# LoRA router, softmax(x @ W): x loaded as float32 by SyncE's queue and converted by ScalarE, weights in few pieces, eight blocks through TensorE at the end

## The chip, the cores and the metric

The kernel runs on one core of a Trainium2 chip. The metric is device time in microseconds (us), the median of several runs. Engines are named as in the profile: PE is TensorE's matmul, PEld its load of the stationary operand, DVE is VectorE, ACT is ScalarE, POOL is GpSimd, SP is SyncE. SPq, ACTq and POOLq are the parts of these engines that issue DMAs. TensorE's granted clock has two levels, 1.2 GHz (0.5 in the profile) and 2.4 GHz (1.0).

## The reference

```python
batch, seq, dim, num_loras = 16, 512, 1024, 8      # x: 33.55 MB of float32
logits = np.matmul(x, router_weights)              # (8192 x 1024) @ (1024 x 8)
exp_logits = np.exp(logits - np.max(logits, axis=-1, keepdims=True))
return exp_logits / np.sum(exp_logits, axis=-1, keepdims=True)
```

## The kernel before

The 8192 rows are split as row = (t, p, g): t is one of T = 4 quarters, p one of 128 partitions, g one of G = 16. A load takes four values of g for one t: 128 partitions x 4 rows x 1024, 2.1 MB of float32 in memory. Four loads (t = 0 to 3) make a group `nb`, and there are NB = 4 groups, so 16 loads in all. The last load (group 3, t = 3) is cut in three (`xl`, two blocks, one, one); a block is one g of one t, 128 rows of x.

x is loaded by POOL's queue, whose DMA converts float32 to bf16 on the way, into nine buffers `xb` (lines 70 to 88); the tenth load waits until a buffer has been read. The weights are loaded by SP's queue (lines 91 to 98): `w_blk` four times, once for each quarter of the partitions, and `w_nat` once. `w_blk` takes word pairs (b, i): partition i holds rows 2 x (32 b + i) and the next, so that each of its 16 pieces is 64 bytes; `w_nat` has eight pieces of 32 bytes on each partition.

DVE then works in the order in which its instructions are written (`tc.manual_schedule`): `wd` is cleared and filled from `w_blk`, `w_bf` from `w_nat`, the identity is copied, `fold` is summed, and after that come the steps for x:

- `turn(nb, t)`: one DVE transpose of 32 x 32 blocks over the whole load, in which a pair of bf16 counts as one float32 word: `xb` to `xt`.
- `logits(nb, nt)`: 32 matmuls with `wd`, in four column strips of TensorE, into `lt`; needs all of the group's transposes.
- `back(nb - 1)`: ACT copies `lt` to `lts`, PE adds the four strips (`po`), and the softmax follows: `mx`, `ex` on DVE, `ev` (Exp) on ACT, `ssum`, `inv`, `outv` on DVE. It is written behind the second transpose of the next group.

The last four blocks go another way: PE transposes each of them in eight steps (`pt`, line 218), DVE copies the result out of PSUM (`xT`, line 220), and `project` multiplies it by `w_bf` in eight steps (line 209) into `lg`. A last softmax and a store by ACT's queue end the kernel.

Of the kernel before, what the change touches and what calls it, by code (L numbers as in the profile page):

```python
# [10 lines left out]
def kernel(  # L11
# [6 lines left out]
    nc = tc.nc  # L18
    P = 128
    B, S, D = x.shape  # L20
    D2, N = router_weights.shape
# [14 lines left out]
    GB = 4  # L36
# [11 lines left out]
    out_tail = out.rearrange("b s n -> (b s) n").rearrange("(t p g) n -> t p g n", t=T, p=P)  # L48
# [5 lines left out]
    xtp = ctx.enter_context(tc.tile_pool(name="xT", bufs=2))  # L54
    sm = ctx.enter_context(tc.tile_pool(name="sm", bufs=2))
    ps_lt = ctx.enter_context(tc.tile_pool(name="ps_lt", bufs=2, space=bass.MemoryType.PSUM))
    ps_out = ctx.enter_context(tc.tile_pool(name="ps_out", bufs=2, space=bass.MemoryType.PSUM))
    ps_t = ctx.enter_context(tc.tile_pool(name="ps_t", bufs=2, space=bass.MemoryType.PSUM))
    ps_lg = ctx.enter_context(tc.tile_pool(name="ps_lg", bufs=1, space=bass.MemoryType.PSUM))

    LAST = NB - 1
    TAIL_LOADS = [2, 1, 1]

    with tc.manual_schedule():

        xs = {}
        tail = []
        ident_bf = const.tile([P, P], bf16)
        ident = const.tile([P, P], fp32)
        for nb in range(NB):  # L70
            for t in range(T):
                if nb == LAST and t == TAIL_T:
                    g = nb * GB
                    for i, r in enumerate(TAIL_LOADS):
                        xb = xtail.tile([P, r, D], bf16, name=f"xl{i}", tag=f"xl{i}")
                        nc.gpsimd.dma_start(out=xb[:], in_=x_v[t, :, g:g + r, :])  # L76
                        tail += [(xb, k) for k in range(r)]
                        g += r
                    continue
                xb = xpool.tile([P, GB, D], bf16, name="xb")  # L80
                if nb == 0 and t == 0:
                    for k in range(GB):
                        nc.gpsimd.dma_start(out=xb[:, k, :], in_=x_v[t, :, k, :])  # L83
                else:
                    nc.gpsimd.dma_start(out=xb[:], in_=x_v[t, :, nb * GB:(nb + 1) * GB, :])  # L85
                xs[nb, t] = xb
                if nb == 0 and t == 0:
                    make_identity(nc, ident)
# [25 lines left out]
        )  # L114

        outv = const.tile([P, Q, G, N], fp32)
        out_t = const.tile([P, GB, N], fp32)

        def softmax(lg, rows, dst, np_):

            shape = [np_] + rows
            ax = X
            mx = sm.tile([P] + rows + [1], fp32, name="mx")
            nc.vector.reduce_max(mx[:np_, ..., 0], lg, axis=ax)  # L124
            ex = sm.tile([P] + rows + [N], fp32, name="ex")
            nc.vector.tensor_tensor(  # L126
                out=ex[:np_], in0=lg, in1=mx[:np_].broadcast_to(shape + [N]), op=ALU.subtract
            )
            ev = sm.tile([P] + rows + [N], fp32, name="ev")
            nc.scalar.activation(ev[:np_], ex[:np_], func=Exp)  # L130
            ssum = sm.tile([P] + rows + [1], fp32, name="ssum")
            nc.vector.reduce_sum(ssum[:np_, ..., 0], ev[:np_], axis=ax)  # L132
            inv = sm.tile([P] + rows + [1], fp32, name="inv")
            nc.vector.reciprocal(inv[:np_], ssum[:np_])  # L134
            nc.vector.tensor_tensor(  # L135
                out=dst, in0=ev[:np_], in1=inv[:np_].broadcast_to(shape + [N]), op=ALU.mult
            )

        xts = {}

        def turn(nb, t):

            if t == 0:
                xts[nb] = tpool.tile([P, T, GB, W], fp32, name="xt")
            nc.vector.transpose(  # L145
                out=xts[nb][:, t].rearrange("p g w -> p (g w)"),
                in_=xs[nb, t][:].rearrange("p g d -> p (g d)").bitcast(fp32),
            )

        def logits(nb, nt):  # L150

            lt = ps_lt.tile([P, T, GB, L], fp32, name="lt")
            xv = xts[nb][:].rearrange("p t g w -> p (t g w)").bitcast(bf16).rearrange(
                "p (t g b l two) -> p t g b l two", t=T, g=GB, b=WB, two=2
            )
# [12 lines left out]

        def back(nb, nt, lt):
            lts = sm.tile([P, GB, T, L], fp32, name="lts")  # L170
            nc.scalar.copy(lts[:, :, 0:nt, :].rearrange("p g t l -> p t g l"), lt[:, 0:nt])  # L171
            po = ps_out.tile([P, GB, Q, N], fp32, name="po")
# [8 lines left out]
            softmax(  # L181
                po[0:nt * L],
                [GB, Q],
                outv[0:nt * L, :, nb * GB:(nb + 1) * GB, :].rearrange("p q g n -> p g q n"),
                nt * L,
            )

        def store(g0, g1, t, eng):
            eng.dma_start(
                out=out_v[t, :, :, g0:g1, :], in_=outv[t * L:(t + 1) * L, :, g0:g1, :]  # L190
            )

        lt = {}
        for nb in range(NB):
            nt = T if nb < LAST else TAIL_T
            for t in range(nt):
                turn(nb, t)
                if t == 1 and nb > 0:
                    back(nb - 1, T, lt.pop(nb - 1))
            lt[nb] = logits(nb, nt)  # L200
        for t in range(T):
            store(0, LAST * GB, t, nc.sync)


        lg = ps_lg.tile([P, GB, N], fp32, name="lg")

        def project(j, xT):
            for ko in range(KO):
                nc.tensor.matmul(  # L209
                    lg[:, j, :], lhsT=xT[:, ko, :], rhs=w_bf[:, ko, :],  # L210
                    start=(ko == 0), stop=(ko == KO - 1),
                )

        pend = None
        for j, (xb, k) in enumerate(tail):
            pt = ps_t.tile([P, KO, P], bf16, name="pt")
            for ko in range(KO):
                nc.tensor.transpose(pt[:, ko, :], xb[:, k, ko * P:(ko + 1) * P], ident_bf[:])  # L218
            xT = xtp.tile([P, KO, P], bf16, name="xT")
            nc.vector.tensor_copy(out=xT[:], in_=pt[:])  # L220
            if pend is not None:
                project(*pend)
            if j == 0:
                back(LAST, TAIL_T, lt.pop(LAST))
                for t in range(TAIL_T):
                    store(LAST * GB, G, t, nc.sync)
            pend = (j, xT)
        project(*pend)
        softmax(lg[:], [GB], out_t[:], P)
        nc.scalar.dma_start(out=out_tail[TAIL_T, :, LAST * GB:G, :], in_=out_t[:])  # L230


# [28 lines left out]
```

## Time and profile before

| | |
|---|---|
| median of 3 runs | 108.58 us (107.95 to 110.44) |
| the profiled execution's own time | 107.87 us |
| its span, first to last instruction | 106.0 us |
| PE, DVE, ACT, POOL busy | 21.7, 44.6, 5.0, 11.9 us |
| memory read, written | 33.72 MB, 0.26 MB |

The profile is of one execution. Its own time is 1.87 us longer than its span, which is what lies ahead of the first and behind the last instruction. Busy time counts compute instructions alone; a DMA's bytes are counted as it writes them, so the loads of x appear there with 16.78 MB (bf16) and in the memory's own row with 33.5 MB (float32).

### The profile page before, as it was taken

The page shows a single profiled execution, that of the slowest core. Times are in us where ns is not written, and L with a number is a line of the kernel's source. Part 1 is how long each engine was busy: PE and PEld are TensorE (multiplying, and loading weights), DVE is VectorE, ACT ScalarE, POOL GpSimd, SP SyncE. Part 2 cuts the span into 40 slices and gives each one's busy share as a digit, 9 for nine tenths or more (in the row PEclk, how much of TensorE's full clock was granted, in tenths as well). Part 3 has the DMA queues.
Part 4 walks back from the last instruction along what each step waited for, and adds up shares of the span by engine and source line. Part 5 has one row for each costly group of instructions (what it writes and reads, how often), then busy time and mean ns, then how long its engine had stood idle before and what let it go on. Part 6 is the DMA issues. An engine that isn't in the chain of part 4 may idle for free.

```text
span 106.0 us, 617 instructions
## 1 busy us (share of the span) xinstructions
PE 21.7 (21%) x224; PEld 12.7 (12%) x224; DVE 44.6 (42%) x52; ACT 5.0 (5%) x10; POOL 11.9 (11%) x27
## 2 busy tenths in 40 slices
PE   0000000000000000000000772039700673099420
PEld 0000000000000000000000332012600222049410
DVE  1210001000000000003999985999289994904750
ACT  4000000000000000000000021000210021002000
POOL 6963100000000000000121127000000000000000
PEclk9999999999999999999999998555555578558855
DMA  2899999999999999992079999999999995300000
GB/s 22 109 194 231 215 215 217 214 214 217 214 214 217 217 211 217 214 214 54 0 102 219 222 201 222 219 207 219 219 207 232 192 207 105 68 7 0 12 6 6
DMA packets 7329, 17.22 MB, mean 162 GB/s; under 512 B 4640, under 2 KB 4640, under 8 KB 5536
## 3 DMA queue, kind: packets, MB, share of 16 engines
q0 software_dynamic: 3024, 16.78, 78.1%
q1 hardware_dynamic: 4160, 0.41, 4.1%
q10 hardware_dynamic: 144, 0.02, 0.1%
q8 instruction: 1, 0.02, 0.1%
HBM read 33.72 MB, written 0.26 MB: 320 GB/s over the span
## 4 chain that ended last, share of the span: by engine, by line
DMA 44%; DVE 28%; PE 19%; ACT 3%; SPq 2%; issue 2%; ACTq 0%; DVEq 0%
DMA w_nat<-in_router_weights_dram 44%; DVE xt L145 19%; PE lt L160 12%; PE po L174 4%; DVE xT L220 2%; PE pt L218 2%; SPq L95 2%; ACT lts L171 2%; ACT ev L130 1%; DVE mx L124 1%; DVE ex L126 1%; DVE ssum L132 1%; DVE inv L134 1%; DVE outv L135 1%; PE lg L209 1%
## 5 line engine op out<-in xcount | busy, mean ns | idle before, releaser
L145 DVE STREAM_TRANSPOSE xt<-xb 128x2048 f32<-128x2048 f32 x15 | 33.3, 2279 | 0.0
L160 PE MATMUL lt<-xt,wd 128*32 128x512 bf16 (+1 forms) x128 | 13.1, 584 | 76.0 <-DVE xt L145 76.0
L160 PEld LDWEIGHTS <-wd 128*32 128x32 bf16 x128 | 4.7, 135 | 81.8 <-issue 52.9
L108 DVE CAST w_bf<-w_nat 128x64 bf16<-128x64 f32 x1 | 0.2, 197 | 31.6 <-DMA w_nat<-in_router_weights_dram 31.6
L85 POOL DMA_DIRECT2D xb<-in_x_dram x14 | 7.4, 534 | 52.7 <-DVE xt L145 50.0
L103 DVE CAST wd<-w_blk 32x256 bf16<-32x256 f32 x4 | 1.3, 324 | 15.2 <-DMA w_blk<-in_router_weights_dram 15.2
L171 ACT COPY lts<-lt 128x512 f32<-128x512 f32 (+1 forms) x4 | 2.2, 558 | 84.4 <-PE lt L160 84.4
L174 PE MATMUL po<-fold,lts 128*128 128x32 f32 (+1 forms) x32 | 5.0, 305 | 2.1 <-ACT lts L171 2.1
L174 PEld LDWEIGHTS po<-fold,lts 128*128 128x128 f32 (+1 forms) x32 | 4.6, 224 | 4.4 <-ACT lts L171 4.4
L220 DVE COPY xT<-pt 128x1024 bf16<-128x1024 bf16 x4 | 2.7, 685 | 4.5 <-PE pt L218 4.5
L218 PE MATMUL pt<-ident_bf,xl 128*128 128x128 bf16 x32 | 3.3, 264 | 0.0
L124 DVE TENSOR_REDUCE mx<-po 128x16 f32<-128x128 f32 (+1 forms) x4 | 1.2, 291 | 3.7 <-PE po L174 3.7
L218 PEld LDWEIGHTS <-xl 128*128 128x128 bf16 x32 | 2.5, 120 | 0.6 <-issue 0.6
L83 POOL DMA_DIRECT2D xb<-in_x_dram x4 | 2.3, 585 | 0.8 <-POOLq L245 0.8
L132 DVE TENSOR_REDUCE ssum<-ev 128x16 f32<-128x128 f32 (+2 forms) x5 | 1.3, 265 | 2.0 <-ACT ev L130 2.0
L130 ACT ACTIVATE ev<-ex 128x128 f32<-128x128 f32 (+2 forms) x5 | 1.5, 293 | 12.7 <-DVE ex L126 12.7
L209 PE MATMUL lg<-w_bf,xT 128*128 128x8 bf16 x32 | 1.5, 170 | 2.1 <-DVE xT L220 2.1
L76 POOL DMA_DIRECT2D xl<-in_x_dram x3 | 1.6, 547 | 0.0
L209 PEld LDWEIGHTS <-xT 128*128 128x128 bf16 x32 | 1.3, 105 | 2.4 <-DVE xT L220 2.4
L171 ACT ACT_TABLE_LOAD x1 | 1.3, 1283 | 0.7 <-PEq L245 0.7
L134 DVE RECIPROCAL inv<-ssum 128x16 f32<-128x16 f32 (+2 forms) x5 | 1.2, 237 | 0.2
L135 DVE TENSOR_TENSOR outv<-ev,inv 128x128 f32<-128x128 f32 (+1 forms) x4 | 1.2, 291 | 0.1
(13 smaller groups left out, 3.8 us busy)
## 6 DMA issues: line engine op xcount, KB each, us to landing
xb<-in_x_dram POOLq DMA_DIRECT2D x14, 1024.0 KB, 18.9
xb<-in_x_dram POOLq DMA_DIRECT2D x4, 256.0 KB, 5.9
xl<-in_x_dram POOLq DMA_DIRECT2D x1, 512.0 KB, 22.7
xl<-in_x_dram POOLq DMA_DIRECT2D x2, 256.0 KB, 24.9
out_dram<-outv SPq DMA_DIRECT2D x4, 48.0 KB, 1.7
w_blk<-in_router_weights_dram SPq DMA_DIRECT2D x4, 32.0 KB, 3.6
out_dram<-outv SPq DMA_DIRECT2D x3, 16.0 KB, 1.5
w_nat<-in_router_weights_dram SPq DMA_DIRECT2D x1, 32.0 KB, 46.7
```

Of the source, the lines that this page charges most:

```text
L83: nc.gpsimd.dma_start(out=xb[:, k, :], in_=x_v[t, :, k, :])
L85: nc.gpsimd.dma_start(out=xb[:], in_=x_v[t, :, nb * GB:(nb + 1) * GB, :])
L124: nc.vector.reduce_max(mx[:np_, ..., 0], lg, axis=ax)
L130: nc.scalar.activation(ev[:np_], ex[:np_], func=Exp)
L132: nc.vector.reduce_sum(ssum[:np_, ..., 0], ev[:np_], axis=ax)
L145: nc.vector.transpose(out=xts[nb][:, t].rearrange("p g w -> p (g w)"), in_=xs[nb, t][:].rearrange("p g d -> p (g d)").bitcast(fp32),)
L160: nc.tensor.matmul(lt[c * L:(c + 1) * L, 0:nt], lhsT=wd[:, b, two, :], rhs=xv[:, 0:nt, :, b, :, two], start=(s < Q), stop=(s >= steps - Q),)
L171: nc.scalar.copy(lts[:, :, 0:nt, :].rearrange("p g t l -> p t g l"), lt[:, 0:nt])
L174: nc.tensor.matmul(po[0:nt * L, g].rearrange("p q n -> p (q n)"), lhsT=lts[:, g, 0:nt, :], rhs=fold[:], start=True, stop=True,)
L209: nc.tensor.matmul(lg[:, j, :], lhsT=xT[:, ko, :], rhs=w_bf[:, ko, :], start=(ko == 0), stop=(ko == KO - 1),)
L218: nc.tensor.transpose(pt[:, ko, :], xb[:, k, ko * P:(ko + 1) * P], ident_bf[:])
L220: nc.vector.tensor_copy(out=xT[:], in_=pt[:])
```

## The change

x is loaded by SP's queue as float32, without conversion, into five buffers `xf` of 2.1 MB. ACT converts each load to bf16 (`cast`, into one of three buffers `xb`) and DVE transposes that. The weights go to ACT's queue, and the words of x are put in another order: pair number (i, b) instead of (b, i), so that `w_blk` has one piece of 1 KB on each partition, and `w_nat` (ki, ko) one of 256 bytes. To match it, the transpose reads words that lie 64 bytes apart, and PE's transposes take columns that lie 16 bytes apart. `TAIL_T` goes from 3 to 2: the last eight blocks (t = 2 and 3 of the last group) go through PE's transposes, ACT converting each block. POOL clears `wd`. `fill` adds matmuls whose result (`spare`) nobody reads: ten ahead of the last group's logits and two behind each of the first five of the eight blocks. The softmax is cut into `peak` (DVE), `power` (ACT) and `share` (DVE), which are written between other steps. All stores are on SP's queue.

```diff
-    TAIL_T = T - 1
+    LAST = NB - 1
+    TAIL_T = 2
...
-    xpool = ctx.enter_context(tc.tile_pool(name="x", bufs=9))
-    xtail = ctx.enter_context(tc.tile_pool(name="xtail", bufs=1))
+    fpool = ctx.enter_context(tc.tile_pool(name="xf", bufs=5))
+    bpool = ctx.enter_context(tc.tile_pool(name="xb", bufs=3))
...
-        wv = router_weights.rearrange("(b i two) n -> i b (two n)", i=L, two=2)
+        wv = router_weights.rearrange("(i b two) n -> i b (two n)", b=WB, two=2)
         for q in range(Q):
-            nc.sync.dma_start(out=w_blk[q * L:(q + 1) * L], in_=wv)
-        nc.sync.dma_start(
-            out=w_nat[:], in_=router_weights.rearrange("(ko ki) n -> ki ko n", ki=P)
+            nc.scalar.dma_start(out=w_blk[q * L:(q + 1) * L], in_=wv)
+        nc.scalar.dma_start(
+            out=w_nat[:], in_=router_weights.rearrange("(ki ko) n -> ki ko n", ko=KO)
         )
...
+        for nb, t, k0, r in loads:
+            xb = fpool.tile([P, GB, D], fp32, name="xf")
+            g = nb * GB + k0
+            nc.sync.dma_start(out=xb[:, 0:r, :], in_=x_v[t, :, g:g + r, :])
...
-        nc.vector.memset(wd[:], 0.0)
+        nc.gpsimd.memset(wd[:], 0.0)
...
+        def cast(nb, t, r=GB):
+            xb = bpool.tile([P, GB, D], bf16, name="xb")
+            for k in range(0, GB, r):
+                src, j = xf[nb, t, k]
+                nc.scalar.copy(xb[:, k:k + r, :], src[:, j:j + r, :])
...
-            nc.vector.transpose(
-                out=xts[nb][:, t].rearrange("p g w -> p (g w)"),
-                in_=xs[nb, t][:].rearrange("p g d -> p (g d)").bitcast(fp32),
-            )
+            for k in range(0, GB, r):
+                nc.vector.transpose(
+                    out=xts[nb][:, t, k:k + r].rearrange("p g b l -> p (g b) l"),
+                    in_=xbs[nb, t][:, k:k + r, :].rearrange("p g d -> p (g d)").bitcast(fp32)
+                    .rearrange("p (g i b) -> p g b i", g=r, i=L),
+                )
...
+            if nb == LAST:
+                fill(10, moving(nb)[:, 0, 0, :, :, 0])
...
-        for j, (xb, k) in enumerate(tail):
+        for j, (t, k) in enumerate(tail):
...
+            nc.scalar.copy(xb[:, k, :], src[:, s, :])
+            xc = xb[:, k, :].rearrange("p (ki ko) -> p ko ki", ko=KO)
...
-                nc.tensor.transpose(pt[:, ko, :], xb[:, k, ko * P:(ko + 1) * P], ident_bf[:])
+                nc.tensor.transpose(pt[:, ko, :], xc[:, ko, :], ident_bf[:])
...
+            if j < len(tail) - 3:
+                fill(2, moving(LAST)[:, 0, 0, :, :, 0])
             if j == 0:
-                back(LAST, TAIL_T, lt.pop(LAST))
+                lts = copy_out(LAST, TAIL_T, lt)
+            if j == 1:
+                sft = back(LAST, TAIL_T, lts)
+            if j == 2:
+                sft.peak()
+            if j == 3:
+                sft.power()
+            if j == 4:
+                sft.share()
```

ACT's program before, its last rows; it has no work on x itself:

```order
L171 COPY lts<-lt 128x4x4x32
L130 ACTIVATE ev<-ex 128x128
L171 COPY lts<-lt 128x3x4x32
L130 ACTIVATE ev<-ex 96x128
L130 ACTIVATE ev<-ex 128x32
L230 DMA out_dram<-out_t 128x32
```

Ahead of these rows stand only the table load and the same pair of copy and Exp, twice.

ACT's program now, its first eight rows (lines 73 and 74 are the weights, line 150 is `cast`, line 196 is the copy of `lt`, line 129 is Exp):

```order
L73 DMA w_blk<-in_router_weights_dram 32x256 x4
L74 DMA w_nat<-in_router_weights_dram 128x64
L150 ACT_TABLE_LOAD
L150 CAST xb<-xf 128x4096 x5
L196 COPY lts<-lt 128x4x4x32
L150 CAST xb<-xf 128x4096
L129 ACTIVATE ev<-ex 128x128
L150 CAST xb<-xf 128x4096 x3
```

The copy of a group's `lt` stands behind the first cast of the next group, and the Exp behind the second; casts that follow wait for both.

ACT's program now, its last rows, from the last group on (line 262 is the cast of one of the last eight blocks):

```order
L150 CAST xb<-xf 128x2048 x2
L196 COPY lts<-lt 128x4x4x32
L150 CAST xb<-xf 128x2048 x2
L129 ACTIVATE ev<-ex 128x128
L262 CAST xb<-xf 128x1024
L196 COPY lts<-lt 128x2x4x32
L262 CAST xb<-xf 128x1024 x3
L129 ACTIVATE ev<-ex 64x128
L262 CAST xb<-xf 128x1024 x4
L129 ACTIVATE ev<-ex 128x64
```

The copy of the last `lt` stands between the first and the second of the eight casts, and the Exp of that group behind the fourth.

DVE's program before, from its last transpose on:

```order
L145 STREAM_TRANSPOSE xt<-xb 128x2048
L220 COPY xT<-pt 128x1024
L124 TENSOR_REDUCE mx<-po 96x16
L126 TENSOR_TENSOR ex<-po,mx 96x128
L132 TENSOR_REDUCE ssum<-ev 96x16
```

The softmax of the last group stands whole behind the first copy out of PSUM.

DVE's program now, from the last two loads that it transposes in halves (line 158 is the transpose, line 268 the copy out of PSUM, lines 120 to 137 the softmax):

```order
L158 STREAM_TRANSPOSE xt<-xb 128x1024 x2
L134 TENSOR_REDUCE ssum<-ev 128x16
L136 RECIPROCAL inv<-ssum 128x16
L137 TENSOR_TENSOR outv<-ev,inv 128x4x4x8
L268 COPY xT<-pt 128x1024 x3
L120 TENSOR_REDUCE mx<-po 64x16
L122 TENSOR_TENSOR ex<-po,mx 64x128
L268 COPY xT<-pt 128x1024 x2
L134 TENSOR_REDUCE ssum<-ev 64x16
```

`mx` and `ex` of the last group, for which ACT's Exp waits, stand behind the third copy out of PSUM.

## Rows read from the trace of the kernel before

**Rows 1.** The page: 40 slices of 2.65 us, DMA's busy tenths and GB/s written.

```profile
DMA  2899999999999999992079999999999995300000
GB/s 22 109 194 231 215 215 217 214 214 217 214 214 217 217 211 217 214 214 54 0 102 219 222 201 222 219 207 219 219 207 232 192 207 105 68 7 0 12 6 6
```

**Rows 2.** The chain that ended last, in order of time: start us, us, what.

```profile
2.75 46.74 DMA w_nat<-in_router_weights_dram
...
50.12 8.81 DVE xt L145 x4
58.97 3.50 PE lt L160 x32
```

**Rows 3.** The waits of all engines: who for whom, us in total, times, longest.

```profile
POOL xb L85 <- DVE xt L145: 50.0, 6, 41.6
```

**Rows 4.** Stretches: length, busy us of each engine, granted clock, DMA share, GB/s written.

```profile
12.00:46.00 34.00, 0.00 (x0) 0.10 (x1) 0.29 (x1) 0.00 (x0) 0.00 (x0) 1.00 1.06 215
...
49.60:53.50 3.90, 0.00 (x0) 0.00 (x0) 3.90 (x5) 0.00 (x0) 0.53 (x1) 1.00 0.00 0
...
56.00:82.00 26.00, 10.07 (x80) 5.23 (x79) 22.19 (x20) 1.79 (x4) 3.69 (x7) 0.68 1.02 214
```

**Rows 5.** The DMA queues: packets, MB written, share of 16 engines' span.

```profile
q0 software_dynamic: 3024, 16.78, 78.1%
```

**Rows 6.** The start in order of time: start us, us, engine, instruction.

```profile
0.74 1.96 SPq L95 DMA_DIRECT2D w_blk<-in_router_weights_dram  x4
1.23 2.27 POOL L83 DMA_DIRECT2D xb<-in_x_dram  x4 [0.78 <-POOLq L245]
2.63 0.44 DVE L103 CAST wd<-w_blk 32x256 bf16<-32x256 f32 x1 [1.23 <-DMA w_blk<-in_router_weights_dram]
3.44 0.26 POOL masks.py:197 MEMSET ident<- 128x128 f32 x1
```

**Rows 7.** Groups by line and shape: busy us, mean ns of one, idle before.

```profile
L130 ACT ACTIVATE ev<-ex 128x128 f32<-128x128 f32 x3 | 0.9, 309 | 6.4 <-DVE ex L126 6.4
L130 ACT ACTIVATE ev<-ex 128x32 f32<-128x32 f32 x1 | 0.2, 229 | 4.5 <-DVE ex L126 4.5
L171 ACT COPY lts<-lt 128x512 f32<-128x512 f32 x3 | 1.8, 585 | 78.3 <-PE lt L160 78.3
L145 DVE STREAM_TRANSPOSE xt<-xb 128x2048 f32<-128x2048 f32 x15 | 33.3, 2279 | 0.0
L112 DVE TENSOR_REDUCE fold<-ident 128x32 f32<-128x128 f32 x1 | 0.4, 364 | 0.0
L132 DVE TENSOR_REDUCE ssum<-ev 128x16 f32<-128x128 f32 x3 | 0.9, 286 | 1.2 <-ACT ev L130 1.2
L218 PEld LDWEIGHTS <-xl 128*128 128x128 bf16 x32 | 2.5, 120 | 0.6 <-issue 0.6
L174 PEld LDWEIGHTS po<-fold,lts 128*128 128x128 f32 x24 | 3.7, 237 | 4.4 <-ACT lts L171 4.4
```

**Rows 8.** The end in order of time: start us, us, engine, instruction.

```profile
92.60 2.75 PE L160 MATMUL lt<-xt,wd 128*32 128x384 bf16 x32 [4.27 <-DVE xt L145]
95.28 1.03 PE L218 MATMUL pt<-ident_bf,xl 128*128 128x128 bf16 x8
...
96.11 0.90 PE L174 MATMUL po<-fold,lts 128*96 128x32 f32 x8
96.35 0.69 DVE L220 COPY xT<-pt 128x1024 bf16<-128x1024 bf16 x1 [3.81 <-PE pt L218]
...
97.50 0.61 PE L218 MATMUL pt<-ident_bf,xl 128*128 128x128 bf16 x8
...
101.67 0.38 PE L209 MATMUL lg<-w_bf,xT 128*128 128x8 bf16 x8 [0.59 <-DVE xT L220]
102.08 0.19 DVE L124 TENSOR_REDUCE mx<-lg 128x4 f32<-128x32 f32 x1 [0.47 <-PE lg L209]
...
103.28 0.19 DVE L135 TENSOR_TENSOR out_t<-ev,inv 128x32 f32<-128x32 f32 x1
```

More of the change, by code (lines that the diff above doesn't have):

```diff
@@ L47 @@
     )
-    out_tail = out.rearrange("b s n -> (b s) n").rearrange("(t p g) n -> t p g n", t=T, p=P)
+    out_tail = out.rearrange("b s n -> (b s) n").rearrange("(t p g) n -> p t g n", t=T, p=P)
     const = ctx.enter_context(tc.tile_pool(name="const", bufs=1))
-    xpool = ctx.enter_context(tc.tile_pool(name="x", bufs=9))
-    xtail = ctx.enter_context(tc.tile_pool(name="xtail", bufs=1))
+    fpool = ctx.enter_context(tc.tile_pool(name="xf", bufs=5))
+    bpool = ctx.enter_context(tc.tile_pool(name="xb", bufs=3))
@@ L59 @@
+    ps_out = ctx.enter_context(tc.tile_pool(name="ps_out", bufs=1, space=bass.MemoryType.PSUM))
+    ps_t = ctx.enter_context(tc.tile_pool(name="ps_t", bufs=4, space=bass.MemoryType.PSUM))
     ps_lg = ctx.enter_context(tc.tile_pool(name="ps_lg", bufs=1, space=bass.MemoryType.PSUM))
-    LAST = NB - 1
-    TAIL_LOADS = [2, 1, 1]
+    ps_f = ctx.enter_context(tc.tile_pool(name="ps_f", bufs=1, space=bass.MemoryType.PSUM))
+    loads = [(nb, t, 0, GB) for nb in range(NB) for t in range(T)]
+    loads[-1:] = [(LAST, T - 1, 0, 2), (LAST, T - 1, 2, 1), (LAST, T - 1, 3, 1)]
@@ L64 @@
     with tc.manual_schedule():
[L66 to L88, printed above, removed]
@@ new lines @@
+        nc.scalar.dma_start(
+            out=w_nat[:], in_=router_weights.rearrange("(ki ko) n -> ki ko n", ko=KO)
+        )
+        xf = {}
+        for nb, t, k0, r in loads:
+            xb = fpool.tile([P, GB, D], fp32, name="xf")
+            g = nb * GB + k0
+            nc.sync.dma_start(out=xb[:, 0:r, :], in_=x_v[t, :, g:g + r, :])
+            for k in range(r):
+                xf[nb, t, k0 + k] = (xb, k)
+        ident = const.tile([P, P], fp32)
+        make_identity(nc, ident)
+        ident_bf = const.tile([P, P], bf16)
@@ L116 @@
         outv = const.tile([P, Q, G, N], fp32)
[L117 to L127, printed above, removed]
-            )
[L129 to L137, printed above, removed]
@@ L139, with __init__, peak, power @@
-        xts = {}
-        def turn(nb, t):
-            if t == 0:
-                xts[nb] = tpool.tile([P, T, GB, W], fp32, name="xt")
-            nc.vector.transpose(
-                out=xts[nb][:, t].rearrange("p g w -> p (g w)"),
-                in_=xs[nb, t][:].rearrange("p g d -> p (g d)").bitcast(fp32),
-            )
+        out_t = const.tile([P, T - TAIL_T, GB, N], fp32)
+        spare = ps_f.tile([P, 512], fp32)
+        class Softmax:
+            def __init__(self, lg, rows, dst, np_):
+                self.lg, self.rows, self.dst, self.np_ = lg, rows, dst, np_
+            def peak(self):
+                n, rows = self.np_, self.rows
+                mx = sm.tile([P] + rows + [1], fp32, name="mx")
+                nc.vector.reduce_max(mx[:n, ..., 0], self.lg, axis=X)
+                self.ex = sm.tile([P] + rows + [N], fp32, name="ex")
+                nc.vector.tensor_tensor(
+                    out=self.ex[:n], in0=self.lg, in1=mx[:n].broadcast_to([n] + rows + [N]),
+                    op=ALU.subtract,
+                )
+            def power(self):
+                self.ev = sm.tile([P] + self.rows + [N], fp32, name="ev")
+                nc.scalar.activation(self.ev[:self.np_], self.ex[:self.np_], func=Exp)
+            def share(self):
+                n, rows = self.np_, self.rows
+                ssum = sm.tile([P] + rows + [1], fp32, name="ssum")
+                nc.vector.reduce_sum(ssum[:n, ..., 0], self.ev[:n], axis=X)
+                inv = sm.tile([P] + rows + [1], fp32, name="inv")
+                nc.vector.reciprocal(inv[:n], ssum[:n])
+                nc.vector.tensor_tensor(
+                    out=self.dst, in0=self.ev[:n], in1=inv[:n].broadcast_to([n] + rows + [N]),
+                    op=ALU.mult,
+                )
@@ L150, in logits @@
         def logits(nb, nt):
             lt = ps_lt.tile([P, T, GB, L], fp32, name="lt")
-            xv = xts[nb][:].rearrange("p t g w -> p (t g w)").bitcast(bf16).rearrange(
-                "p (t g b l two) -> p t g b l two", t=T, g=GB, b=WB, two=2
-            )
+            xv = moving(nb)
             steps = 2 * WB
@@ L167, in logits, with moving, fill, copy_out @@
             return lt
-        def back(nb, nt, lt):
+        def moving(nb):
+            return xts[nb][:].rearrange("p t g b l -> p (t g b l)").bitcast(bf16).rearrange(
+                "p (t g b l two) -> p t g b l two", t=T, g=GB, b=WB, two=2
+            )
+        def fill(n, rhs, k=None):
+            for _ in range(n):
+                nc.tensor.matmul(
+                    spare[:], lhsT=w_fill, rhs=rhs, start=True, stop=True
+                )
+        w_fill = wd[:, 0:2].rearrange("p b two n -> p (b two n)")
+        def copy_out(nb, nt, lt):
             lts = sm.tile([P, GB, T, L], fp32, name="lts")
             nc.scalar.copy(lts[:, :, 0:nt, :].rearrange("p g t l -> p t g l"), lt[:, 0:nt])
+            return lts
+        def back(nb, nt, lts):
             po = ps_out.tile([P, GB, Q, N], fp32, name="po")
@@ L180, in back @@
                 )
-            softmax(
+            return Softmax(
                 po[0:nt * L],
@@ L196 @@
             for t in range(nt):
[L197 to L200, printed above, removed]
+                r = 2 if nb == LAST else GB
+                cast(nb, t, r)
+                if lt is not None:
+                    if t == 0:
+                        sft = back(nb - 1, T, copy_out(nb - 1, T, lt))
+                    if t == 1:
+                        sft.power()
+                turn(nb, t, r)
@@ L201 @@
+                if lt is not None:
+                    if t == 0:
+                        sft.peak()
+                    if t == 1:
+                        sft.share()
+                        lt = None
+            if nb == LAST:
+                fill(10, moving(nb)[:, 0, 0, :, :, 0])
+            lt = logits(nb, nt)
         for t in range(T):
-            store(0, LAST * GB, t, nc.sync)
-        lg = ps_lg.tile([P, GB, N], fp32, name="lg")
-        def project(j, xT):
+            store(t, 0, LAST * GB)
@@ L208, in project @@
+        tail = [(t, k) for t in range(TAIL_T, T) for k in range(GB)]
+        lg = ps_lg.tile([P, T - TAIL_T, GB, N], fp32, name="lg")
+        def project(t, k, xT):
             for ko in range(KO):
                 nc.tensor.matmul(
-                    lg[:, j, :], lhsT=xT[:, ko, :], rhs=w_bf[:, ko, :],
+                    lg[:, t - TAIL_T, k, :], lhsT=xT[:, ko, :], rhs=w_bf[:, ko, :],
                     start=(ko == 0), stop=(ko == KO - 1),
                 )
-        pend = None
-        for j, (xb, k) in enumerate(tail):
+        pend = []
@@ L216 @@
+        for j, (t, k) in enumerate(tail):
+            if k == 0:
+                xb = bpool.tile([P, GB, D], bf16, name="xb")
+            src, s = xf[LAST, t, k]
+            nc.scalar.copy(xb[:, k, :], src[:, s, :])
+            xc = xb[:, k, :].rearrange("p (ki ko) -> p ko ki", ko=KO)
             pt = ps_t.tile([P, KO, P], bf16, name="pt")
             for ko in range(KO):
-                nc.tensor.transpose(pt[:, ko, :], xb[:, k, ko * P:(ko + 1) * P], ident_bf[:])
+                nc.tensor.transpose(pt[:, ko, :], xc[:, ko, :], ident_bf[:])
@@ L219 @@
             xT = xtp.tile([P, KO, P], bf16, name="xT")
             nc.vector.tensor_copy(out=xT[:], in_=pt[:])
-            if pend is not None:
-                project(*pend)
-            if j == 0:
-                back(LAST, TAIL_T, lt.pop(LAST))
-                for t in range(TAIL_T):
[L226 to L230, printed above, removed]
+            pend.append((t, k, xT))
@@ new lines @@
+            if len(pend) > 1:
+                project(*pend.pop(0))
+            if j < len(tail) - 3:
+                fill(2, moving(LAST)[:, 0, 0, :, :, 0])
+            if j == 0:
+                lts = copy_out(LAST, TAIL_T, lt)
+            if j == 1:
+                sft = back(LAST, TAIL_T, lts)
+            if j == 2:
+                sft.peak()
+            if j == 3:
+                sft.power()
+            if j == 4:
+                sft.share()
+                for t in range(TAIL_T):
+                    store(t, LAST * GB, G)
@@ L234 @@
+        for p in pend:
+            project(*p)
+        end = Softmax(lg[:], [T - TAIL_T, GB], out_t[:], P)
+        end.peak()
+        end.power()
+        end.share()
+        nc.sync.dma_start(
+            out=out_tail[:, TAIL_T:, LAST * GB:G, :].rearrange("p t g n -> p t (g n)"),
+            in_=out_t[:].rearrange("p t g n -> p t (g n)"),
+        )
 _INS = ['x', 'router_weights']
```

17 lines of the change are left out of this document (10 added, 7 removed).

## Prediction

> **What bounds the kernel now.** I read the 40 slices first [rows 1]. DMA is busy nearly throughout to slice 18, drops to nothing for about 4 us, and is busy again to slice 33: two stretches of loading with a hole between. The chain [rows 2] says what made the hole: the last weight transfer, `w_nat`, lands 46.74 us after its issue, and only then does DVE begin the transposes at 50.12. Meanwhile the nine buffers were full, and POOL's next load waited 41.6 us for a transpose [rows 3]; from 49.6 to 53.5 nothing was written [rows 4]. Behind the hole DVE is busy 22.19 of 26 us and DMA is full too [rows 4], so the second half is as long as its loads, and the tail comes on top. The bytes themselves: 215 GB/s written in bf16 from 12 to 46 us [rows 4] are 430 GB/s read, and 33.55 MB at that rate take 78.0 us. So some 28 us of the span of 106.0 are not loading: about 2 at the start, about 5 in and around the hole, the rest at the end.
>
> **x as float32 through SP's queue.** SP issues its first load where the weights went out before, at 0.74 [rows 6], with about 0.5 us an issue; the weights' first piece was used 1.5 us after the issue, so bytes flow from about 1.8 us. The read rate is known, but each byte read is now a byte written, and the trace shows no such transfer. The fast end is the read rate of [rows 4], 78.0 us. The slow end that I keep in the range is the time that the packets of x took, 78.1% of 106.0 = 82.8 us (405 GB/s) [rows 5]. I take 80.0, near the first, since the stretch in mid-stream is a pure stream of the same reads: 5.0 us for each 2.1 MB. The weights add 0.16 MB, 0.4 us. With about 1.0 us from the last byte to its use, the last block has landed at T = 1.8 + 80.0 + 0.4 + 1.0 = 83.2 us.
>
> The Trainium skill ("DMA: Bandwidth & Descriptors", "Where 436 GB/s comes from") says that a load from HBM is bound by some 358 GB/s per core; 33.55 MB would then take 93.7 us instead of 80.0; the skill's "HBM Reference", "Specifications (TRN2)", gives a core that streams alone about 425, which would be 78.9. The trace speaks for the second as far as reads go: 430 GB/s [rows 4].
>
> **ACT converts.** From Exp at 128 and at 32 elements, 309 and 229 ns [rows 7], one element costs 0.833 ns; 4096 take 0.31 + 3968 x 0.833 = 3.61 us, 2048 take 1.91, 1024 take 1.06. bf16 output I take at the same rate. In a group ACT has four casts (14.4), one copy of `lt` (0.59) and one Exp (0.31). The copy stands behind the next group's first cast and waits for the transpose (2.28) and the logits (3.50) that follow the fourth cast: 5.8 against the 3.6 that the first cast covers, so some 2.2 us idle. Together 17.5 us a group, against 20.0 of loading. ACT keeps up with 2.5 to spare; five float32 buffers hide what it is late by. This cover is gone if the transpose costs over 4.8 us.
>
> **Weights.** Before, 3072 pieces (2048 of 64 bytes, 1024 of 32) ended at 49.5 us. Now there are 256 pieces. By pieces that is 46.74 x 256 / 3072 = 3.9 us, twice that if each waits for a piece of x that is twice as long to write: 4 to 8 us. By bytes it would be the old 46.7. I take 8 and `w_nat` at about 11, since the bytes are few and the pieces were many. DVE starts two loads late and makes up 2.3 us or more with each load: no cost. By the order of the changed program five of SP's loads also wait for a weight transfer (the ninth for `w_nat`); SP reaches the ninth only when the fourth cast is done, at about 26 us. POOL's clearing of `wd` is eight times the 0.26 us of [rows 6], done at about 4: hidden behind the weights.
>
> **The transpose reads words 64 bytes apart.** The nearest row by instruction is the old transpose, 2279 ns; by pattern it is the sum for `fold`, which reads words 128 bytes apart: 364 ns against 286 for as many elements side by side [rows 7], 0.61 ns more for each. On 2048 that is 3.5 us. Either is below the 4.8 above. I take 2.3 and keep 3.5 for the range (0.6 us at the end, where halves are transposed).
>
> The Trainium skill ("Advanced Engine Details and Errata", "SBUF Cachelines") has a rule against this layout: accesses that each touch another 16-byte line pay a penalty. It names no size; the `fold` row, 364 against 286 ns, is at least in its direction. By the rule the sum is that of the strided rival below.
>
> **The end, after T.** Load t = 1 of the last group lands at T - 10, t = 2 at T - 5. The two half casts are done at T - 6.2, the last half transposed (1.2) at T - 5.0, and the logits of 256 columns (2.75 x 256 / 384 = 1.83 [rows 8]) at T - 3.2. The ten fills ahead of them run while PE would wait. ACT: first block cast by T - 3.9, waits for `lt`, copies it (0.37) by T - 2.8, casts blocks 2, 3 and 4 by T + 0.4, and stands before Exp. PE per block: eight transposes, 1.03 us in the slow case and 0.61 in the fast [rows 8], I take 0.8; `project` 0.38; two fills of 512 columns, 0.43 each at 1.2 GHz (3.50 / 8 [rows 2], four side by side) and half at 2.4, I take 0.3. So PE: block 1 at T - 2.4, fills to -1.8; block 2 to -0.9, project, fills to +0.1; `po` (0.90 [rows 8], taken as 1.0) to +1.1; block 3 to +1.9. DVE copies it (0.69) to 2.6 and makes `mx` and `ex` (0.6) by 3.2; only then ACT's Exp, to 3.5, and the four casts that queue behind it: T + 7.8. PE meanwhile: block 4 with project and fills to 4.7, block 5 to 6.5, block 6 to 7.7, block 7 to 8.9, block 8 transposed at 9.7. Copy and last project: 10.8. PE, not ACT, ends last, by about 1 us. The last softmax took 1.4 us [rows 8]; with twice the columns 1.6: T + 12.4. From there to the end of the span it took 106.0 - 103.47 = 2.5: T + 14.9.
>
> **The sum.** 83.2 + 14.9 = 98.1 us of span, and 1.87 around it: 100.0. The profiled run before was 107.87, 0.7 under the median of 108.58; I add nothing for that. Before, the last load ended at about 90 us [rows 1] and 16 us followed; now 83.2 and 14.9: the gain is the hole and the late start of the transposes, not the tail.
>
> **Rivals.**
> Strided reads cost. PE's loads of columns 16 bytes apart have no row; between the plain bf16 load, 120 ns, and the float32 load of the same 128 columns, 237 [rows 7], eight of them add up to 0.94 us a block. PE ends last, so eight blocks add 7.5: 107.5 us, no change. For it: every column lies on its own. Against: loads lie beside the matmuls.
>
> Slower: the write side is the limit. Nothing in the trace writes more than 232 GB/s [rows 1]; at that rate x takes 145 us. Slower than before by 2% (110.8) it is from 90.8 us of loading on, that is below 370 GB/s; midway between 232 and 430 it is 101 us of loading and 121 in all. Against it: the old rate is just what reading gives at a busy share of 1.0, and the engines were halving the bytes, not queueing them. By the 358 GB/s of the Trainium skill ("DMA: Bandwidth & Descriptors", as above) the time would be 113.7 us.
>
> Slower too: the transpose at 5.0 us or more, 2.2 times the old. DVE would then go from 13 us on through 14 transposes with 0.4 of softmax each (75.6), end at 88.6, and the logits (1.8), the 18.1 us from their end to that of the span (T - 3.2 to T + 14.9) and 1.9 around it give 110.4. It is over twice the surplus of `fold`.
>
> Weights late as before: `w_nat` at 46.7, ACT stopped after three casts; eleven casts at 4.4 from 48.5 on, then 20 us of tail: about 119. It decides from 26 us on.
>
> **How the numbers follow.** The forecast, DMA bound with a tail of PE, has 0.78: 100.0, from 96 (78.0 us of load and PE at 2.4 GHz, -2.0 and -2.5) to 104.5 (82.8 of load, or all PE at 1.2 GHz, +2.8 and +3.2, not both in full). Strided loads of PE: 0.12, from 104.5 to 109, half of it within 2%. Write side: 0.05. Slow transpose: 0.03. Weights: 0.02. A measurement can tell about 2% here (2.2 us; three runs spread by 2.5). Faster: 0.78 + 0.06 = 0.84. Same: 0.06, and 0.02 of the write side: 0.08. Slower: 0.08. The range reaches from 96 to 107.5 and leaves out the slower cases and the worst of the strided one.
>
> **What the profile after would show.** Right: GB/s near 420 without a hole from the third slice to about 82 us; a cast of 4096 elements near 3.6 us; `w_nat` landed before 15 us; ACT idle between casts for DMA, not for DVE; at the end PE's blocks 1.2 to 1.8 us apart, and ACT waiting some 2.5 us before the Exp of the last group. Wrong: GB/s under 380, a transpose over 4.8 us, loads of 16-byte-apart columns over 200 ns, or ACT's casts waiting for DVE in mid-stream. The surest term is the removed wait for `w_nat`; the least sure are the write rate and PE's pace at the end.

## The result, and the profile after

| | before | changed |
|---|---|---|
| median of 4 runs | 109.17 us (107.95 to 110.44) | 99.95 us (99.81 to 100.36) |
| ratio to before | | 0.924 [0.917, 0.930] |
| the profiled execution's span | 106.0 us | 97.9 us |

Ratios, here and below, leave out runs more than 1.5% above the fastest of the same kernel, while the medians are of all runs. Predicted were 100.0 us and a span of 98.1. The first thing to look at is the loading. The page of the changed kernel, 40 slices of 2.45 us, and its rows of queues:

```profile
ACT  0504939494949279969492799694927945729410
DMA  3899999999999999999999999999999996100000
GB/s 87 348 435 397 403 430 423 428 428 428 428 428 428 428 428 428 428 428 428 428 428 428 428 428 428 428 428 428 428 428 422 402 408 231 23 7 0 13 0 13
...
q1 hardware_dynamic: 3728, 33.82, 82.8%
```

The hole of [rows 1] is gone: DMA is busy from the second slice to the thirty-third. The rate is 428 GB/s, now of bytes that are read and written alike; before it was 430 read and half of that written [rows 4]. The last bytes of x come at about 82 us (predicted 82.2). The weights, which the chain before waited for [rows 2], no longer stop the loading. The start of the changed kernel in order of time, ACT and DVE:

```profile
0.73 2.17 ACTq L73 DMA_DIRECT2D w_blk<-in_router_weights_dram  x4
...
2.94 0.45 ACTq L74 DMA_DIRECT2D w_nat<-in_router_weights_dram  x1
...
8.75 3.60 ACT L150 CAST xb<-xf 128x4096 bf16<-128x4096 f32 x1 [4.06 <-DMA xf<-in_x_dram]
...
16.43 0.20 DVE L99 CAST w_bf<-w_nat 128x64 bf16<-128x64 f32 x1 [4.76 <-DMA w_nat<-in_router_weights_dram]
```

`w_nat` is there at 16.4 us and not at 49.5. DVE begins its transposes at 17, when two loads have landed and the first cast has been done for 4.6 us. By 32.4 it has caught up: there it waits for a cast for the first time. Groups by line and shape of the changed kernel (mean ns behind the bar), to set against [rows 7]:

```profile
L158 DVE STREAM_TRANSPOSE xt<-xb 128x2048 f32<-128x2048 f32 x12 | 43.6, 3652 | 4.4 <-ACT xb L150 4.3
L150 ACT CAST xb<-xf 128x4096 bf16<-128x4096 f32 x12 | 43.2, 3604 | 12.5 <-DMA xf<-in_x_dram 12.5
L158 DVE STREAM_TRANSPOSE xt<-xb 128x1024 f32<-128x1024 f32 x4 | 7.7, 1971 | 0.0
L266 PEld LDWEIGHTS <-xb 128*128 128x128 bf16 x64 | 5.3, 152 | 2.7 <-ACT xb L262 1.8 <-issue 0.4
```

The cast costs what was worked out (3.61). The transpose costs 3.65 us and not 2.28. ACT's idle time ahead of its casts is put down to DMA: in mid-stream the loads are the bound. In the stretch from 82.4 to 95 us PE ran at a mean granted clock of 0.91, so mostly at 2.4 GHz (length, busy us of each engine, clock, DMA share, GB/s):

```profile
82.40:95.00 12.60, 9.69 (x142) 7.38 (x140) 7.28 (x17) 7.04 (x9) 0.00 (x0) 0.91 0.07 16
```

The end in order of time, where columns are start us, us, engine, instruction:

```profile
74.47 3.70 ACT L150 CAST xb<-xf 128x2048 bf16<-128x2048 f32 x2
...
76.40 3.74 DVE L158 STREAM_TRANSPOSE xt<-xb 128x1024 f32<-128x1024 f32 x2
...
80.20 1.62 PE L172 MATMUL lt<-xt,wd 128*32 128x256 bf16 x32 [2.24 <-DVE xt L158]
...
81.88 0.37 ACT L196 COPY lts<-lt 128x256 f32<-128x256 f32 x1 [1.91 <-PE lt L172]
82.15 2.94 ACT L262 CAST xb<-xf 128x1024 bf16<-128x1024 f32 x3
...
87.49 0.31 ACT L129 ACTIVATE ev<-ex 64x128 f32<-64x128 f32 x1 [2.40 <-DVE ex L122]
87.71 3.87 ACT L262 CAST xb<-xf 128x1024 bf16<-128x1024 f32 x4
...
88.79 0.71 PE L266 MATMUL pt<-ident_bf,xb 128*128 128x128 bf16 x8 [0.76 <-ACT xb L262]
...
93.76 0.23 DVE L120 TENSOR_REDUCE mx<-lg 128x8 f32<-128x64 f32 x1 [0.45 <-PE lg L252]
```

ACT stands 2.40 us before the last group's Exp, as foreseen, with four casts behind it. The last softmax begins at 93.76 (predicted 83.2 + 10.8 = 94.0).

### The profile page after: what moved, and what is told of

It reads as the page before. It is cut to its first block, busy times and chain, and to the rows that moved or that the text cites. A ratio compares the mean times of both kernels' runs of the same rounds, so it can differ in the third digit from the quotient of the medians.

```text
span 97.9 us, 820 instructions
## 1 busy us (share of the span) xinstructions
PE 29.8 (30%) x308; PEld 17.8 (18%) x308; DVE 64.2 (66%) x56; ACT 62.4 (64%) x34; POOL 1.6 (2%) x7
## 3 DMA queue, kind: packets, MB, share of 16 engines
q1 hardware_dynamic: 3728, 33.82, 82.8%
## 4 chain that ended last, share of the span: by engine, by line
DMA 34%; DVE 28%; PE 16%; ACT 14%; issue 3%; ACTq 2%
DVE xt L158 22%; DMA xf<-in_x_dram 21%; DMA w_nat<-in_router_weights_dram 14%; ACT xb L150 12%; PE lt L172 9%; PE pt L266 4%; DVE xT L268 3%; ACTq L73 2%; PE spare L188 1%; ACT xb L262 1%; PE lg L252 1%; ACT ev L129 1%; PE po L202 1%; DVE ex L122 1%; DVE inv L136 0%
## 5 line engine op out<-in xcount | busy, mean ns | idle before, releaser
L150 ACT CAST xb<-xf 128x4096 bf16<-128x4096 f32 (+1 forms) x16 | 50.6, 3178 | 13.8 <-DMA xf<-in_x_dram 13.8
L158 DVE STREAM_TRANSPOSE xt<-xb 128x2048 f32<-128x2048 f32 (+1 forms) x16 | 51.3, 3232 | 4.5 <-ACT xb L150 4.3
L268 DVE COPY xT<-pt 128x1024 bf16<-128x1024 bf16 x8 | 5.4, 688 | 5.8 <-PE pt L266 5.8
L262 ACT CAST xb<-xf 128x1024 bf16<-128x1024 f32 x8 | 7.9, 1043 | 0.5 <-DMA xf<-in_x_dram 0.5
L266 PE MATMUL pt<-ident_bf,xb 128*128 128x128 bf16 x64 | 6.1, 245 | 0.8 <-ACT xb L262 0.8
L188 PE MATMUL spare<-xt,wd 128*128 128x512 bf16 x20 | 5.9, 411 | 0.0
L266 PEld LDWEIGHTS <-xb 128*128 128x128 bf16 x64 | 5.3, 152 | 2.7 <-ACT xb L262 1.8
L252 PE MATMUL lg<-w_bf,xT 128*128 128x8 bf16 x64 | 2.8, 167 | 0.9 <-DVE xT L268 0.9
L252 PEld LDWEIGHTS <-xT 128*128 128x128 bf16 x64 | 2.4, 97 | 1.1 <-DVE xT L268 1.1
L188 PEld LDWEIGHTS <-wd 128*128 128x128 bf16 x20 | 1.7, 105 | 1.0
## 6 DMA issues: line engine op xcount, KB each, us to landing
w_nat<-in_router_weights_dram ACTq DMA_DIRECT2D x1, 32.0 KB, 13.5
```

Source lines behind the costliest of these rows:

```text
L150: nc.scalar.copy(xb[:, k:k + r, :], src[:, j:j + r, :])
L158: nc.vector.transpose(out=xts[nb][:, t, k:k + r].rearrange("p g b l -> p (g b) l"), in_=xbs[nb, t][:, k:k + r, :].rearrange("p g d -> p (g ...
L188: nc.tensor.matmul(spare[:], lhsT=w_fill, rhs=rhs, start=True, stop=True)
L252: nc.tensor.matmul(lg[:, t - TAIL_T, k, :], lhsT=xT[:, ko, :], rhs=w_bf[:, ko, :], start=(ko == 0), stop=(ko == KO - 1),)
L262: nc.scalar.copy(xb[:, k, :], src[:, s, :])
L266: nc.tensor.transpose(pt[:, ko, :], xc[:, ko, :], ident_bf[:])
```

## The experiments

The theory after the result: all of the gain is that the weights land before the loading runs out of buffers (A). The rival: float32 through SP's queue, the conversion on ACT or the eight blocks carry part of it (B). Beside each run the kernel before ran on the same chip, with medians of 108.67 us (runs 1 to 4), 109.32 (runs 5, 6, 8, 9) and 108.70 (runs 7, 10); the ratios are to it. The changed kernel was not run beside them, so a difference to its 99.95 us is given by the medians and, where that says something else, by the ratios.

**1. The weights in few pieces alone.** The kernel before with the new word order, nothing else:

```diff
-        wv = router_weights.rearrange("(b i two) n -> i b (two n)", i=L, two=2)
+        wv = router_weights.rearrange("(i b two) n -> i b (two n)", b=WB, two=2)
...
-            out=w_nat[:], in_=router_weights.rearrange("(ko ki) n -> ki ko n", ki=P)
+            out=w_nat[:], in_=router_weights.rearrange("(ki ko) n -> ki ko n", ko=KO)
...
-                in_=xs[nb, t][:].rearrange("p g d -> p (g d)").bitcast(fp32),
+                in_=xs[nb, t][:].rearrange("p g d -> p (g d)").bitcast(fp32)
+                .rearrange("p (g i b) -> p g b i", g=GB, i=L),
```

> The kernel before with one part of the change alone: the word order in which the weights lie in few pieces (and the transposes on VectorE and TensorE that read accordingly); x still comes as bf16 through GpSimd's queue, weights on SyncE's queue, four blocks through TensorE at the end. Theory A (all of the gain is that w_nat no longer lands at 49.5 us and the loading has no hole): w_nat at 10 to 18 us, GB/s written near 215 without a hole, the last load landed near 82 us, 97 to 100 us. Rival B (float32 through SyncE's queue, conversion on ScalarE or the eight blocks carry part of it): 103 us or more.

Measured: 98.36 us (98.11 to 99.03), ratio 0.909 [0.902, 0.916]. That is 1.6 us less than the whole change. Its page and its start in order of time:

```profile
GB/s 23 133 193 224 216 216 216 216 216 213 216 216 216 216 216 216 216 213 219 213 216 213 219 213 216 216 216 216 216 213 219 197 207 215 51 0 0 20 0 7
...
8.71 0.20 DVE L108 CAST w_bf<-w_nat 128x64 bf16<-128x64 f32 x1 [1.64 <-DMA w_nat<-in_router_weights_dram]
...
9.93 3.60 DVE L145 STREAM_TRANSPOSE xt<-xb 128x2048 f32<-128x2048 f32 x1 [0.62 <-DMA xb<-in_x_dram]
```

No hole, weights at 8.7 us, the transposes 50.1 - 9.9 = some 40 us earlier than in [rows 2], although each now takes 3.6 us. A stands; this one part gives no less than the whole, and 1.6 us more by the medians.

**2. The old word order in the changed kernel.** The same edit the other way:

> The changed kernel with the old word order: weights in 3072 pieces again, transposes of words side by side; all else as changed. Theory A (pieces decide when the weights land): w_nat lands after 40 us again, the casts stop after three, and the time is 112 to 130 us. Rival B (it is the queue, or x as float32, that lets the weights through): w_nat before 20 us, transposes 2.3 us, 97 to 99 us.

Measured: 100.46 us (99.30 to 101.15), ratio 0.920 [0.910, 0.930]: neither. The weights land at 19 us although they are in 3072 pieces. Stretches of this kernel (length, busy us of each engine, clock, DMA share, GB/s), its start, and SP's own waits:

```profile
4.00:17.00 13.00, 0.00 (x0) 0.00 (x0) 0.00 (x0) 1.43 (x2) 0.00 (x0) 1.00 1.01 425
17.00:20.00 3.00, 0.00 (x0) 0.00 (x0) 0.89 (x4) 3.00 (x1) 0.00 (x0) 1.00 0.83 68
...
0.73 14.25 ACTq L73 DMA_DIRECT2D w_blk<-in_router_weights_dram  x4
...
SPq L83 <- DMA w_blk<-in_router_weights_dram: 16.8, 1, 16.8
```

A load on SP's queue waits 16.8 us for a weight transfer; by the bytes moved until then it is the fourth. When the first three loads were through, the stream stopped for about 3 us (68 GB/s), and in that gap the weights landed. So more pieces do take longer beside x (all landed by about 20 us against 16.4, and that with an empty stream to help), but SP's wait in the changed kernel's own order keeps them from coming last. The gap cost about 2.5 us of loading. That the faster transposes (2.31 us; run 5 prices them) gave it back fits the time, but was not tried apart.

**3. The weights first, old order, old queues.** In the kernel before, the weights are issued ahead of x, and POOL copies a few values of each weight tile before its first load:

```diff
+        hold = const.tile([P, 2 * N], fp32)
+        nc.gpsimd.tensor_copy(out=hold[:], in_=w_blk[:, 0, :])
+        nc.gpsimd.tensor_copy(out=hold[:, 0:N], in_=w_nat[:, 0, :])
...
         nc.gpsimd.dma_start(out=xb[:, k, :], in_=x_v[t, :, k, :])
```

> The kernel before, old word order and old queues; GpSimd copies a word of w_blk and of w_nat ahead of its first load, so that x waits until the weights have landed. Theory A: weights landed by 6 to 8 us, x streams from then on without a hole, the last load at 85 to 87 us, 97.5 to 101 us, although neither the pieces nor the conversion have changed. Rival B: 104 us or more.

Measured: 100.78 us (100.11 to 101.31), ratio 0.929 [0.920, 0.939]. Its page and its start:

```profile
GB/s 17 49 13 154 204 237 211 215 218 215 221 211 211 211 218 211 215 225 218 211 215 215 218 218 215 211 211 218 211 221 218 218 200 202 220 20 0 20 7 7
...
5.07 0.20 DVE L111 CAST w_bf<-w_nat 128x64 bf16<-128x64 f32 x1 [0.24 <-DMA w_nat<-in_router_weights_dram]
...
5.68 2.25 POOL L95 DMA_DIRECT2D xb<-in_x_dram  x4 [0.33 <-issue]
```

With nothing beside them the same 3072 pieces are there at 5 us. The loading starts 4.4 us late and has no hole; the whole kernel is as fast as the changed one, within the intervals. A again, with neither pieces nor conversion changed.

**4. Without the fills.** The changed kernel, `fill` left out at both places.

> The changed kernel without its twenty fill matmuls. Theory A: TensorE's clock at the end is lower, but its eight blocks are paced by ScalarE's casts and by the wait for the Exp of the last group; within 0.7 us of the changed kernel's 99.95. Rival: the clock was worth it, 1.5 to 3 us slower. (Third: the fills stood in the way, 1 us faster.)

Measured: 100.44 us (99.45 to 100.96), ratio 0.924 [0.916, 0.933] against 0.924 for the changed kernel: no difference in the time to be seen. In the four runs of the changed kernel the mean granted clock was 0.964, 0.881, 0.778 and 0.785, and the times were 99.99, 99.91, 100.36 and 99.81: the clock does not order them. In the four runs without fills it does: 0.928, 0.825, 0.824 and 0.722 went with 99.45, 100.44, 100.45 and 100.96 us. In the two traces the granted clock from 82.4 to 95 us was 0.91 with fills and 0.64 without, and yet the last softmax began at 93.76 and at 93.97. That the fills raise the clock is not shown by this: the traces of runs 8 and 9, with and without fills, have 0.88 and 0.86 from 82 to 94 us.

**5. Words side by side.** The changed kernel, the transpose reading `p (g b i)` in place of `p (g i b)`. It leaves out the reordering of x's words, so x meets other weights and only the time is of use.

> The changed kernel with VectorE's transposes reading words side by side, weights still in few pieces; this leaves out the reordering of the words, so that x's words meet other weights. It prices the 64-byte step alone. The transpose should take 2.3 us instead of 3.65. Theory A (the step costs only where VectorE is late, at the start and for the two half transposes ahead of the last logits): 97.5 to 99.3 us, 0.6 to 2.5 less than the changed kernel. Rival (loading covers all of it): 99.5 to 100.4 us.

Measured: 98.24 us (97.62 to 98.86), ratio 0.899 [0.892, 0.905]: the 64-byte step costs 1.7 us of the 99.95 (2.7 by the ratios, 2.4 between the spans of the two traces). The row behind it, and ACT at the end:

```profile
L158 DVE STREAM_TRANSPOSE xt<-xb 128x2048 f32<-128x2048 f32 x12 | 27.6, 2306 | 19.9 <-ACT xb L150 19.9
...
73.03 3.70 ACT L150 CAST xb<-xf 128x2048 bf16<-128x2048 f32 x2
...
79.80 0.37 ACT L196 COPY lts<-lt 128x256 f32<-128x256 f32 x1
```

The last half casts begin at 73.03 and the last logits are there by 79.80, against 74.47 and 81.88 in the changed kernel.

**6. The last group's Exp behind the casts.**

```diff
-            if j == 3:
+            if j == 7:
                 sft.power()
-            if j == 4:
                 sft.share()
                 for t in range(TAIL_T):
```

The sums and the stores of that group move with the Exp.

> The changed kernel with the last group's Exp, its sums and its stores moved behind the last of the eight blocks, so that ScalarE does not stand 2.4 us before that Exp with four casts queued behind it. Theory A (ScalarE's queue paces the end): casts 5 to 8 some 2.4 us earlier, 97.7 to 99 us. Rival B (TensorE's eight blocks pace the end, as predicted): casts earlier, but blocks 5 to 8 only 0 to 1 us earlier, 99.2 to 100.2 us.

Measured: 98.97 us (98.80 to 99.03), ratio 0.905 [0.901, 0.909]. The casts of blocks 2 to 8 now follow each other, and PE is not kept waiting:

```profile
81.67 6.74 ACT L262 CAST xb<-xf 128x1024 bf16<-128x1024 f32 x7
...
87.60 0.65 PE L266 MATMUL pt<-ident_bf,xb 128*128 128x128 bf16 x8
...
88.75 0.65 PE L266 MATMUL pt<-ident_bf,xb 128*128 128x128 bf16 x8
89.23 0.34 PE L252 MATMUL lg<-w_bf,xT 128*128 128x8 bf16 x8
```

1.0 us of the 2.4 comes back by the medians (2.0 by the ratios): the wait was on the path, and behind it PE and DVE were nearly as late. Block 5 begins 1.2 us earlier (87.60 against 88.79) and the last `project` 1.5 us (91.88 against 93.37), of which DVE's sums of that group, now ahead of the last softmax, take part back. The time is at the upper end of A's range; the blocks moved little more than B has it.

**7. Four blocks instead of eight**, `TAIL_T = 3` in the changed kernel.

> The changed kernel with four blocks through TensorE at the end instead of eight (t = 2 of the last group transposed by VectorE again, the last group's Exp behind the fourth block). If the eight blocks are worth something here: the half casts and half transposes of t = 2 (3.7 and 1.9 us) and longer logits (2.75) stand on the path, 100.5 to 103 us. Rival (eight blocks on ScalarE and TensorE take as long as they save): 99.3 to 100.4 us.

Measured: 99.28 us (98.88 to 99.92), ratio 0.922 [0.914, 0.930]: the rival's time, just under its range. Eight blocks save nothing that can be seen where ACT has to convert each.

**8. The DMA converts.** The changed kernel, x again as bf16 through POOL's queue into ten buffers, no casts:

```diff
-            xb = fpool.tile([P, GB, D], fp32, name="xf")
+            xb = fpool.tile([P, GB, D], bf16, name="xf")
-            nc.sync.dma_start(out=xb[:, 0:r, :], in_=x_v[t, :, g:g + r, :])
+            nc.gpsimd.dma_start(out=xb[:, 0:r, :], in_=x_v[t, :, g:g + r, :])
...
-            nc.scalar.copy(xb[:, k, :], src[:, s, :])
-            xc = xb[:, k, :].rearrange("p (ki ko) -> p ko ki", ko=KO)
+            xc = src[:, s, :].rearrange("p (ki ko) -> p ko ki", ko=KO)
```

POOL makes the identity ahead of its loads here, and DVE clears `wd`.

> The changed kernel with one part undone: x comes as bf16 through GpSimd's queue (ten buffers), no casts on ScalarE; weights, word order, eight blocks and fills as changed. Theory A (the conversion on ScalarE gains nothing in the stream and costs at the end): GB/s read about 430 as with float32, the last load near 82 us, 94 to 97.5 us. Rival B (float32 through SyncE's queue is worth something in the stream): 100.5 us or more.

Measured: 95.87 us (94.57 to 97.11), ratio 0.873 [0.866, 0.881]: 4.1 us less than with the conversion on ACT (5.5 by the ratios). The stream is as fast: 215 GB/s written from 10 to 70 us, 430 read. The chain of this kernel (start us, us, what):

```profile
73.53 3.68 DVE xt L153 x2
77.21 0.04 issue
77.25 1.79 PE lt L167 x24
79.04 1.01 PE pt L258 x8
```

The last group's second load is transposed as it lands, at 73.53; in the changed kernel the same load is cast from 74.47 and transposed from 76.40, and its logits start at 80.20 instead of 77.25. Of those 3 us the cast of one half is 1.9; the rest is mostly ACT standing before the copy of `lt`, since the same cast began at 73.03 in run 5. The 3 us, and the 1 us of run 6 behind the logits, are where the conversion on ACT costs time.

**9. The same without the fills.**

> As the run with the DMA converting, and without the twenty fill matmuls. With no cast to wait for, TensorE has four blocks waiting when the last logits are done, and ten fills stand between them. If TensorE paces this end: 1 to 3 us less than with fills, 92.5 to 96 us. If the higher clock that fills give is worth as much: the same within 0.7 us.

Measured: 95.35 us (94.57 to 96.05), ratio 0.870 [0.863, 0.877], the fastest of all; 0.5 less than with fills is inside the intervals. Its weights, in 256 pieces on ACT's queue beside x written as bf16:

```profile
2.56 10.98 DMA w_nat<-in_router_weights_dram
```

**10. The same with four blocks.**

> The DMA converting, no fills, four blocks through TensorE instead of eight. No cast stands in front of TensorE here, so eight blocks are only TensorE's and VectorE's time. From the run with eight (last load of t = 2 near 78.5 us): transposes to 82.2, logits to 84.9, four blocks to 89.2, 94 us of span: 95.5 to 97 us, about 1 us over the 95.35 with eight. Rival (four blocks less are four us less behind the logits): 92 to 94.5 us.

Measured: 96.99 us (96.61 to 97.35), ratio 0.900 [0.892, 0.907]. Where no cast stands ahead, eight blocks are worth 1.6 us by the medians and 3.2 by the ratios, on two chips.

## Why the prediction was right, point by point

- **What bounds the kernel; the removed wait.** Right, and shown by runs 1 and 3: each takes away the late landing of the weights, in two different ways, leaves x on its old path and has the whole gain (98.36 and 100.78 against 99.95). "The gain is the hole and the late start of the transposes, not the tail" holds: x's last bytes came by about 89 us before and by 82 now, which is 7 of the 8 us of span; 17 and 16 us followed. (Of the 28 us before that were not loading, the prediction puts some 21 at the end in one place and 16 in another; it was 17.) The prediction didn't say that the rest of the change might have a negative sum. Against run 1 it has, by 1.6 us.
- **The write rate.** 80.0 us were taken, between 78.0 and 82.8. Mid-stream ran at 428 GB/s, which is 78.4 us for x. The fast end was right as a rate: a byte written beside each byte read cost nothing. The whole stream still took the 80 us that were forecast, from about 2 to about 82, since it was below 428 GB/s in most slices up to 17 us and in the last four. The rival of the write side fell. So did, for a core that runs alone, the 358 GB/s of the Trainium skill ("DMA: Bandwidth & Descriptors", "Where 436 GB/s comes from"). The 425 of the Trainium skill's "HBM Reference" ("Specifications (TRN2)") agrees with the 428 here.
- **ACT converts.** 3.61 predicted, 3604 ns measured; 2.2 us idle before the copy of `lt` predicted, 2.53, 2.48 and 2.36 measured. That this came so near is partly luck: the transpose was 1.4 us longer than taken, and the cast that covers it waits some 1.3 us for its load and so ends later. In the stream it is covered, as said. That it isn't covered at the end stood in the working of the tail, but was not set against leaving the conversion to the DMA, so its 4.1 us (run 8) went unsaid.
- **The weights.** About 11 us taken, 16.4 measured. The rule used (by pieces, a piece of x between each two) gave 4 us beside x written as bf16 and 8 beside float32; measured from the last issue to landing it was 6.1 us in run 1 and 13.5 in the changed kernel, so the size was 1.6 times too small. The factor of two looks right from these two, but the same pieces on ACT's queue beside x as bf16 took 11.0 in run 9; what part of the 13.5 comes from the wider writes and what from the queue and the order of issue is open. The late landing cost nothing that the stream shows: 428 GB/s in every slice from the eighth to the thirtieth. The rival "weights late as before, 119 us" was wrong as priced: run 2 makes them late by their pieces, and SP's own wait for `w_blk` stops x after three loads, lets them land at 19 to 20 us and costs about 2.5 us. The prediction names such waits of SP, but leaves them out of this rival.
- **The transpose.** The term that was mis-sized. 2.3 us taken, 3.5 kept for the range; 3.65 measured, 0.67 ns more for each word, against 0.61 from the `fold` row. That row was the right one to take. Priced at 0.6 us for the slow case, the step cost 1.7 (run 5): it acts not only on the last halves but also on the group before, for whose `lt` ACT waits. That the sum came out within 0.1 us is luck: the last logits were 1.8 us late, and what follows them was 2.1 us shorter than taken (see the end). The Trainium skill's rule ("Advanced Engine Details and Errata", "SBUF Cachelines") has the right sign for DVE.
- **PE's loads 16 bytes apart.** 120 ns taken, 237 the bound; 152 measured as a mean over both clock levels, 72 against 57 ns for each where the clock was high (0.58 us for eight, 0.46 before). The rival that gave it 7.5 us fell.
- **The end.** Last logits done at 80.0 predicted, 81.8 measured, by the transposes: with words side by side they are there by 79.8 (run 5). From there to the last softmax 14.0 us were taken, and 11.9 measured. PE went faster than taken, 0.65 to 0.71 us for eight transposes from the third block on, at a granted clock of 0.91, so that ACT's wait before the Exp, not PE, set block 5; "PE, not ACT, ends last" was half right, and run 6 gives the wait 1.0 us. The last softmax began 0.2 us from the predicted time, by the two errors that offset each other.
- **Fills.** Priced as PE time; run 4 shows no effect on the time either way, although in the traces the clock at the end was 0.91 with them and 0.64 without.

## What to carry to other kernels

Beside the running stream the same 0.16 MB of weights had landed 46.7 us after their last issue in 3072 pieces, and 6.1 to 13.5 us after it in 256: the number of pieces matters there, and the bytes alone say little. Count the pieces of whatever the first compute instruction waits for, and let it go first or in few pieces. A conversion that is hidden in the stream by a faster engine is not hidden at the end: here it cost some 4 us there (runs 6 and 8). Before moving work from a DMA to an engine, work out the end both ways. When a change has several parts, try the one part that removes the wait alone: here it gave at least as much as all together, and the version with the good parts (run 9) beats both kernels by 4.6 and some 14 us.

## What was not expected of the hardware

- A load of float32 through SP's queue and a load that converts to bf16 through POOL's ran at the same read rate, 428 and 430 GB/s: halving the bytes written bought nothing for one core.
- DVE's transpose of 128 x 2048 words in blocks of 32 x 32 took 3652 ns with words 64 bytes apart, against 2279 side by side, 1.6 times.
- In run 2 four issues of many small pieces on ACT's queue took 14.25 us, in the changed kernel 2.17 with few. What stands behind them on the engine (here the table load, until 15.6 us) waited with them. The same many pieces took 1.96 us to issue on SP's queue in the kernel before [rows 6], where x came through POOL's queue; which part of the difference makes them wait was not tried.
